# A split-float feed-forward on one NeuronCore: both parts of x in one 512-wide moving operand, the second matrix's operands split on chip

## The chip, the cores and the metric

The program runs on one core of a Trainium2 chip. The metric is the device time of one execution in microseconds (us). The runs of the kernel before took 2144.7, 2146.0 and 2149.2 us; their median, 2146.04 us, is the time before.

## What is computed

One block of a trunk over 512 tokens of width 2048: a projection into four groups of mixers, the mixers, an output projection, and a feed-forward with a squared ReLU. The change lies in the feed-forward and in what borders on it:

```python
x = x + rms_norm(mix @ w_out, norm_mix_post)
h = rms_norm(x, norm_ff_pre)
y = jnp.square(jax.nn.relu(h @ w_ff1)) @ w_ff2        # 2048 -> 8192 -> 2048
x = x + rms_norm(y, norm_ff_post)
```

Everything is float32.

## The kernel before

**Split operands.** Every large product is made from operands that are split in two: `h`, the value rounded to the matmul type (`F32R`), and `l`, the rest. A product of two split operands is three matmuls into one PSUM bank: h times h, h times l, l times h (`mm3`). Splitting takes a cast on ScalarE (`S.copy`) and a subtraction on VectorE.

**Seven products in place of eight.** Each of the two matrices of the feed-forward is multiplied by a Strassen-like scheme: the operands are cut into 2x2 blocks, sums of blocks are made on VectorE (or by accumulating DMAs that GpSimd issues), and seven products p = 1 to 7 are added up into four results. The products are done in the order 1, 5, 6, 2, 7, 3, 4 or close to it; several products go on in a bank where another left off (`PREV`: 6 after 1, 7 after 6, 4 after 7, 3 after 5), once that bank has been read.

**First matrix** (`NU1` = 32 units, about 842 to 1507 us). The weights are the stationary operand, x the moving one. x stands in SBUF as `R` (products 1, 2, 4, 5) and as `S3`, `S6`, `S7` (products 3, 6, 7), with the h part and the l part 256 tokens wide each. One product of one unit is 8 steps of k, and each step is three matmuls with 256 columns: `wh` by x's h, `wh` by x's l, `wl` by x's h. Of the first 16 units the products 1 and 2 are done ahead of the rest (`head_job`, the "heads"); `head_mid` and `head_out` copy the two results to `hst` and send them to DRAM (`stash`). Then come the remaining products (`ffn`, `evac1`); `evac1` squares the ReLU, makes the block sums of y for the second matrix, splits them into h and l, and writes both parts to DRAM (`ydr`, 1792 KB for a unit).

**Second matrix** (`NU2` = 16 units, about 1498 to 2118 us). The parts of y are loaded from `ydr` into regions of `R` (`load_y`, 1024 KB for each product of each pair of units) and are the stationary operand; the weights are the moving one, 512 wide. One product is 24 matmuls. `evac2` adds each finished bank to one of four accumulators (`acc`) on VectorE.

**End.** When a chunk of 512 columns of a token tile is complete, `z_chunk` sums its squares on ScalarE. `final` turns the sum into a factor (`rsq`: VectorE, then a power on GpSimd), multiplies factor and weight row in on VectorE, and adds each chunk to the output in DRAM with an accumulating DMA issued by GpSimd. The residual x had been written to the output earlier, by `x2_tail`.

**What sets the order.** A driver (`Driver`) runs all of this as tasks while the program is built, with a table of instruction costs, and writes an instruction when its task is due. On each engine and each DMA queue the instructions then run in the order written. Weights come as 512 KB blocks through rings of buffers (`V` with three, `X`, `W` and `Z` with two); `mill` adds blocks, casts them to `wh` and subtracts to `wl`, four of each (`NHL`). All helpers record their instructions at line 79, so that the profile tells groups apart by tile names: `R`, `S`, `wh`, `wl`, `raw` (ring V and early weights), `hst`, `ev`, `yt`, `acc`, and `mx` and `pj` for the PSUM banks.

## Time and profile before

| | |
|---|---|
| median of three runs | 2146.04 us |
| the profiled execution, its own time | 2144.77 us |
| its span, first to last instruction | 2142.7 us |
| TensorE busy | 2085.7 us (97%) |
| VectorE busy | 1581.3 us (74%) |
| ScalarE busy | 1071.1 us (50%) |
| GpSimd busy | 218.7 us (10%) |
| DMA, mean | 201 GB/s |

The profile is of one execution. A matmul's row gives its start and a modelled length that reaches into the next one, so the rate of a stream of matmuls is read from the starts of its rows, and a busy share of 97% holds short gaps as well. A row of a table by stretches gives the stretch, its length, and then for TensorE, its weight loads (PEld), VectorE, ScalarE and GpSimd the busy time with the number of instructions; last come the granted TensorE clock as a share of 2.4 GHz, the busy share of the DMA engines, and GB/s. An entry with "x2" or "x4" in a list in order of time is that many instructions in a row, with the time from the first start to the last end. "A <- B" in a list of waits: A sat idle until B ended; the figures are the time in total, the number of waits and the longest.

### The profile page before, as it was taken

How to read it: one execution, taken by the hardware profiler on the slowest of the kernel's cores; microseconds unless marked ns; L12 is line 12 of the kernel's file. 1: busy time of each engine (PE TensorE's matmuls, PEld its weight loads, DVE VectorE, ACT ScalarE, POOL GpSimd, SP SyncE). 2: the span in 40 equal slices, each digit the busy share in tenths (PEclk: the TensorE clock that was granted, in tenths of full speed). 3: DMA queues.
4: the chain of work that ended last, by engine and by line, in shares of the span. 5: the costliest groups of instructions: out<-in, count | busy, mean ns of one | idle time of the engine just before them, and what ended most of it. 6: DMA issues, size and time to landing. Idle time of an engine off the chain costs nothing.

```text
span 2142.7 us, 30890 instructions
## 1 busy us (share of the span) xinstructions
PE 2085.7 (97%) x12100; PEld 1834.5 (86%) x12100; DVE 1581.3 (74%) x2069; ACT 1071.1 (50%) x1530; POOL 218.7 (10%) x280
## 2 busy tenths in 40 slices
PE   9899999999999999989999999999999999999995
PEld 7688888888888888989999999999788888888884
DVE  4655677678765575868888888888667877778775
ACT  6254454465654455645656656656543433433342
POOL 0321121030110000000000000000100100001013
PEclk9999999999999999999999999999999999999998
DMA  8222222222224766677788877788998798789875
GB/s 317 64 90 83 80 74 79 69 79 80 79 79 165 251 227 233 205 247 241 249 252 253 251 243 256 256 258 288 316 310 264 206 305 274 221 256 286 257 209 98
DMA packets 141490, 431.33 MB, mean 201 GB/s; under 512 B 12305, under 2 KB 18721, under 8 KB 136865
## 3 DMA queue, kind: packets, MB, share of 16 engines
q1 hardware_dynamic: 115856, 307.71, 39.9%
q0 software_dynamic: 16128, 54.53, 14.8%
q10 hardware_dynamic: 9360, 67.12, 8.6%
q8 instruction: 95, 1.56, 0.3%
q14 instruction: 51, 0.41, 0.1%
HBM read 358.00 MB, written 71.31 MB: 200 GB/s over the span
## 4 chain that ended last, share of the span: by engine, by line
PE 83%; DMA 5%; DVE 5%; ACT 3%; issue 2%; POOL 1%; SPq 0%; ACTq 0%; POOLq 0%; DVEq 0%
PE mx L79 51%; PE pj L79 32%; DVE wl L79 2%; ACT wh L79 1%; DMA stash<-hst 1%; DMA ydr<-yt 1%; DMA R<-ydr 1%; DVE raw L79 1%; ACT yt L79 0%; DMA raw<-in_w_cv_dram 0%; POOL out_dram L79 0%; DVE yt L79 0%; DMA rsd<-rs 0%; DVE xT L79 0%; DMA wst<-in_ws_t_dram 0%
## 5 line engine op out<-in xcount | busy, mean ns | idle before, releaser
L79 DVE TENSOR_TENSOR wl<-raw,wh 128x1024 fp32r<-128x1024 f32 (+1 forms) x433 | 528.8, 1228 | 332.1 <-ACT wh L79 327.0
L79 ACT CAST wh<-raw 128x1024 fp32r<-128x1024 f32 (+1 forms) x433 | 450.7, 1047 | 574.5 <-DVE raw L79 251.7
L79 PE MATMUL mx<-wh,R 128*128 128x512 f32 x2048 | 644.5, 393 | 7.8 <-ACT wh L79 5.0
L79 PE MATMUL pj<-R,wh 128*128 128x512 f32 (+1 forms) x1888 | 526.3, 362 | 8.7 <-ACT hst L79 8.7
L79 PEld LDWEIGHTS mx<-wh,R 128*128 128x128 f32 x2048 | 387.9, 190 | 88.4 <-ACT wh L79 5.0
L79 PE MATMUL mx<-wl,R 128*128 128x512 f32 x1024 | 402.7, 393 | 1.6 <-DVE wl L79 0.9
L79 PEld LDWEIGHTS pj<-R,wh 128*128 128x128 f32 x1888 | 331.8, 189 | 54.5 <-ACT hst L79 10.6
L79 PE MATMUL pj<-R,wl 128*128 128x512 f32 (+1 forms) x944 | 342.0, 362 | 0.7 <-DVE wl L79 0.7
L79 PE MATMUL mx<-R,wh 128*128 128x256 f32 x1440 | 260.9, 283 | 0.0
L79 PEld LDWEIGHTS mx<-wl,R 128*128 128x128 f32 x1024 | 194.0, 189 | 45.4 <-DVE wl L79 5.1
L79 PE MATMUL mx<-S,wh 128*128 128x256 f32 x1280 | 228.9, 281 | 0.4 <-ACT mx L79 0.4
L79 PEld LDWEIGHTS mx<-R,wh 128*128 128x128 f32 x1440 | 224.5, 192 | 0.0
L79 PE MATMUL mx<-R,wl 128*128 128x256 f32 x720 | 203.9, 283 | 0.0
L79 PEld LDWEIGHTS pj<-R,wl 128*128 128x128 f32 x944 | 178.8, 189 | 23.4 <-DVE wl L79 1.1
L79 PEld LDWEIGHTS mx<-S,wh 128*128 128x128 f32 x1280 | 196.4, 189 | 0.6 <-ACT mx L79 0.6
L79 PE MATMUL mx<-S,wl 128*128 128x256 f32 x640 | 180.4, 282 | 1.2 <-DVE wl L79 1.2
L79 PE MATMUL pj<-wh,R 128*128 128x512 f32 x512 | 162.7, 389 | 0.0
L79 PEld LDWEIGHTS mx<-R,wl 128*128 128x128 f32 x720 | 138.1, 192 | 0.0
L79 DVE TENSOR_TENSOR yt<-yt 128x256 f32<-128x256 f32 (+1 forms) x160 | 113.4, 742 | 32.5 <-ACT yt L79 31.4
L79 POOL DMA_DIRECT2D raw<-in_w_ff_dram x64 | 55.4, 866 | 725.9 <-DVE wl L79 725.9
L79 PEld LDWEIGHTS mx<-S,wl 128*128 128x128 f32 x640 | 120.8, 189 | 2.0 <-DVE wl L79 2.0
L79 PEld LDWEIGHTS pj<-wh,R 128*128 128x128 f32 x512 | 96.1, 188 | 19.9
(292 smaller groups left out, 2462.2 us busy)
## 6 DMA issues: line engine op xcount, KB each, us to landing
ydr<-yt ACTq DMA_DIRECT2D x32, 1792.0 KB, 6.7
R<-ydr SPq DMA_DIRECT2D x56, 1024.0 KB, 10.1
raw<-in_w_ff_dram SPq DMA_DIRECT2D x96, 512.0 KB, 4.6
raw<-in_w_f_dram SPq DMA_DIRECT2D x80, 512.0 KB, 3.3
raw<-in_w_out_dram SPq DMA_DIRECT2D x64, 512.0 KB, 4.1
X<-in_w_ff_dram SPq DMA_DIRECT2D x64, 512.0 KB, 6.2
Z<-in_w_ff_dram SPq DMA_DIRECT2D x64, 512.0 KB, 6.8
raw<-in_w_ff_dram POOLq DMA_DIRECT2D x64, 512.0 KB, 5.8
```

The source lines that it names most:

```text
L79: r = f(*args, **kw)
```

## The change

**First matrix.** `mm1` makes two matmuls of a step instead of three: `wh` by both parts of x, one moving operand of 512 columns (two runs of 256), and `wl` by x's h, 256 columns into the lower half of the bank. A bank so holds two halves that must be added; that is done when it is read (`fold`, and pairs of additions in `evac1`). Because every product now fills a whole bank, results go on in another way: after product 1 its bank is copied by ScalarE into a fresh bank, in which product 2 goes on; after product 6 likewise, with the sign turned, for product 3. A bank that has not yet been written by a matmul gets one first (`seed`). The late product 4 of the unit before now comes after product 6 of a unit, or after product 5 at the first unit of the second matrix, and no longer after its first product.

**Heads.** `head_mid` copies the whole bank (512 columns) to `h1` and sends it off at once; `head_out` folds into `h2` and sends that. `stash` holds three rows for a unit instead of two.

**y.** `ydr` holds y's block sums unsplit (896 KB for a unit, sent in two parts). `load_ys` loads 512 KB for each product into one of two buffers `yr`, in one fixed sequence, the next but one when a buffer has been split; `split_y` casts and subtracts into `R`.

**Weights.** `mill` hands each block to a task of its own (`piece`), so that a block that waits doesn't hold the next ones.

**End.** `z_chunk` multiplies the weight row in at once. In `final`, for the token tiles 0 and 1, ScalarE applies the factor and GpSimd issues the accumulating DMAs as before. For the tiles 2 and 3 the residual is written to a DRAM tile `x2d` early, loaded back into SBUF during the last units (`load_x3`, 1024 KB each), and added on chip, one chunk by ScalarE and GpSimd and three by VectorE; SyncE sends plain writes.

The core of the diff:

```diff
+    x2d = dp.tile([SEQ, D], F32, name="x2d")
...
-            nc.scalar.dma_start(out=out[t * P:(t + 1) * P, c], in_=x2[:, c])
+            nc.scalar.dma_start(out=(out if t < 2 else x2d)[t * P:(t + 1) * P, c], in_=x2[:, c])
...
-        return R[:, hf, hl, off + k, :]
+        return R[:, hf, :, off + k, :]
...
-        seq2 += [(u, todo[0])] + late + [(u, p) for p in todo[1:]]
+        at = todo.index(6) + 1 if u < NU1 else 2
+        seq2 += [(u, p) for p in todo[:at]] + late + [(u, p) for p in todo[at:]]
...
     def mm1(bank, p, k, wh, wl, first, last, on):
-        yield from mm3(bank.t[:, 0:256], wh[:, k, :], wl[:, k, :], op1(p, 0, k), op1(p, 1, k), first, last, on)
+        for low in (True, False) if last else (False, True):
+            if low:
+                T.matmul(out=bank.t[:, 0:256], lhsT=wl[:, k, :], rhs=op1(p, k)[:, 0, :], start=False, stop=False,
+                         skip_group_check=True)
+            else:
+                T.matmul(out=bank.t, lhsT=wh[:, k, :], rhs=op1(p, k), start=first, stop=last, skip_group_check=on)
+            yield PE0
...
+    def fold(dst, bt):
+        S.copy(out=dst, in_=bt[:, 0:256])
+        V.tensor_tensor(out=dst, in0=bt[:, 256:512], in1=dst, op=ALU.add)
...
     def head_mid(u, bank, ev):
         yield ev
-        hst[u] = stage.tile([P, 2, 256], F32, tag="hst", name="hst", bufs=3 if p3 is None else 2)
-        S.copy(out=hst[u][:, 1, :], in_=bank.t[:, 0:256])
+        if p3 is None:
+            x = p2.tile([P, 512], F32, tag="h1", name="h1", bufs=3)
+        else:
+            x = yp.tile([P, 4, 256], F32, tag="yr", name="h1", bufs=2)[:, 0:2].rearrange("p a t -> p (a t)")
+        S.copy(out=x, in_=bank.t)
         hmid[u].fire(drv.cur.time)
+        nc.scalar.dma_start(out=stash[u, :, 1:3, :].rearrange("p a t -> p (a t)"), in_=x)
...
         e, bt = evs[u], banks[u, p][0].t[:, 0:256]
-        if p in (1, 5, 6):
-            S.copy(out=e[:, {1: 0, 5: 1, 6: 2}[p], :], in_=bt)
+        if p in (1, 6):
+            q = {1: 2, 6: 3}[p]
+            yield ("pe", 1)
+            b = Bank()
+            seed(b)
+            banks[u, q] = [b]
+            yield PE0
+            S.activation(out=b.t, in_=bt, func=AF.Copy, scale=1.0 if p == 1 else -1.0)
             mid[u, p].fire(drv.cur.time)
...
-            yh, yl = (y[:, 1:8, hl, :] for hl in range(2))
-            S.copy(out=yh.bitcast(F32R), in_=yl)
-            V.tensor_tensor(out=yl, in0=yl, in1=yh, op=ALU.subtract)
...
+            nc.scalar.dma_start(out=ydr[u, :, 3:7], in_=yb[:, 1:5])
...
+    def load_ys():
+        for n, (b, p) in enumerate(yseq):
+            if n > 1:
+                yield yused[yseq[n - 2]]
+            for u in range(4 * b, 4 * b + 4):
+                yield yfin[u]
+            yield PE0
+            t = yp.tile([P, 4, 256], F32, tag="yr", name="yr", bufs=2)
+            nc.sync.dma_start(out=t, in_=ydr[4 * b:4 * b + 4, :, YI[p]].rearrange("k p t -> p k t"))
+            yraw[b, p] = t
+            ygot[b, p].fire(drv.dma(1 << 19))
+
+    def split_y(b, p, guard):
         yield guard
...
+        S.copy(out=h, in_=t)
+        V.tensor_tensor(out=l, in0=t, in1=h.bitcast(F32), op=ALU.subtract)
+        yload[b, p].fire(drv.cur.time)
+        yused[b, p].fire(drv.cur.time)
...
+        V.tensor_tensor(out=z, in0=z, in1=wfp[:, cs], op=ALU.mult)
...
-            V.scalar_tensor_tensor(out=z, in0=z, scalar=rs, in1=wfp[:, cs], op0=ALU.mult, op1=ALU.mult)
-            G.dma_start(out=out[t * P:(t + 1) * P, cs], in_=z, accum_op=ALU.add)
+            if t < 2:
+                S.activation(out=z, in_=z, func=AF.Copy, scale=rs)
+                yield PE0
+                G.dma_start(out=out[t * P:(t + 1) * P, cs], in_=z, accum_op=ALU.add)
+            elif c == 0:
+                S.activation(out=z, in_=z, func=AF.Copy, scale=rs)
+                G.tensor_tensor(out=z, in0=z, in1=x3s[t][:, cs], op=ALU.add)
+                nc.sync.dma_start(out=out[t * P:(t + 1) * P, cs], in_=z)
+            else:
+                V.scalar_tensor_tensor(out=z, in0=z, scalar=rs, in1=x3s[t][:, cs], op0=ALU.mult, op1=ALU.add)
+                nc.sync.dma_start(out=out[t * P:(t + 1) * P, cs], in_=z)
```

TensorE at the first head of the first matrix, before; `pj` is the bank, `R` holds x, and "x2" stands for two equal instructions:

```order
L79 MATMUL mx<-wh,R 128x512
L79 MATMUL pj<-R,wh 128x256 x2
L79 MATMUL pj<-R,wl 128x256
L79 MATMUL pj<-R,wh 128x256 x2
L79 MATMUL pj<-R,wl 128x256
```

The same place after the change:

```order
L79 MATMUL mx<-wh,R 128x512
L79 MATMUL pj<-R,wh 128x512
L79 MATMUL pj<-R,wl 128x256
L79 MATMUL pj<-R,wh 128x512
L79 MATMUL pj<-R,wl 128x256
```

Two of the three matmuls of a step became one of twice the width; the third stayed.

ScalarE in one unit of the second matrix whose partner unit came before it, that is in every second unit, before:

```order
L79 CAST wh<-raw 128x1024 x8
L79 CAST wh<-W 128x1024 x2
L79 CAST wh<-X 128x1024 x2
L79 CAST wh<-Z 128x1024 x2
L79 CAST wh<-raw 128x1024 x8
```

and after:

```order
L79 CAST wh<-raw 128x1024 x7
L79 CAST R<-yr 128x4x256
L79 COPY mx<-pj 128x512 x2
L79 CAST wh<-W 128x1024
L79 CAST wh<-raw 128x1024
L79 CAST R<-yr 128x4x256
L79 CAST wh<-W 128x1024
L79 CAST wh<-X 128x1024
L79 CAST R<-yr 128x4x256
L79 CAST wh<-X 128x1024
L79 CAST wh<-Z 128x1024
L79 CAST R<-yr 128x4x256
```

The casts of y (`R<-yr`, seven for each pair of units, all in the second one) now stand between the casts of the weights, as does the copy from bank to bank after product 1.

GpSimd at the end, from the power of token tile 2 on, before (`w` and `zs` hold the factor of a token tile, `acc` the chunks, `x` the residual):

```order
L79 TENSOR_TENSOR w_18800<-w_18800,nhalf 128x1
L79 DMA out_dram<-acc_14389 128x512
L79 DMA out_dram<-acc_14390 128x512 x2
L79 DMA out_dram<-acc_14388 128x512 x2
L79 TENSOR_TENSOR w_18820<-w_18820,nhalf 128x1
L79 DMA out_dram<-acc_14390 128x512 x2
L79 DMA out_dram<-acc_14388 128x512 x2
```

and after:

```order
L79 TENSOR_TENSOR zs_7790<-zs_7790,nhalf 128x1
L79 DMA out_dram<-acc_12879 128x512
L79 TENSOR_TENSOR acc_12880<-acc_12880,x_16956 128x512
L79 DMA out_dram<-acc_12879 128x512 x2
L79 TENSOR_TENSOR zs_7791<-zs_7791,nhalf 128x1
L79 TENSOR_TENSOR acc_12880<-acc_12880,x_16958 128x512
```

Of sixteen accumulating DMAs eight are left; behind the power of the last tile GpSimd has one addition where it had four DMAs to issue.

## Rows read from the trace of the kernel before

**Rows 1.** The page: busy time by engine, granted clock, chain that ended last.
```profile
PE 2085.7 (97%) x12100; PEld 1834.5 (86%) x12100; DVE 1581.3 (74%) x2069; ACT 1071.1 (50%) x1530; POOL 218.7 (10%) x280
...
PEclk9999999999999999999999999999999999999998
...
PE 83%; DMA 5%; DVE 5%; ACT 3%; issue 2%; POOL 1%; SPq 0%; ACTq 0%; POOLq 0%; DVEq 0%
```

**Rows 2.** Table by stretches: heads, first matrix, transition, second matrix, end.
```profile
842.00:953.00 111.00, 101.19 (x823) 98.74 (x822) 81.40 (x100) 61.21 (x106) 3.02 (x4) 1.00 0.68 230
953.00:1498.00 545.00, 543.78 (x4559) 543.03 (x4560) 467.37 (x519) 334.23 (x441) 27.82 (x32) 1.00 0.80 252
1498.00:1535.00 37.00, 34.25 (x159) 28.49 (x158) 26.24 (x28) 19.61 (x23) 3.45 (x4) 0.96 1.04 351
1535.00:2107.00 572.00, 571.38 (x2513) 471.20 (x2512) 439.49 (x468) 229.03 (x239) 51.81 (x60) 1.00 0.83 253
2107.00:2142.70 35.70, 11.03 (x49) 8.81 (x47) 16.47 (x31) 5.18 (x13) 17.37 (x20) 0.72 0.71 118
```

**Rows 3.** TensorE in order of time, first matrix: start, length, engine, operation, tiles.
```profile
1100.02 0.40 PE L79 MATMUL mx<-R,wh 128*128 128x256 f32 x2
...
1110.10 0.40 PE L79 MATMUL mx<-R,wh 128*128 128x256 f32 x2
...
1110.46 0.40 PE L79 MATMUL mx<-S,wh 128*128 128x256 f32 x2
...
1118.98 0.40 PE L79 MATMUL mx<-R,wh 128*128 128x256 f32 x2
```

**Rows 4.** TensorE in order of time, projection: x in two runs, 512 wide.
```profile
640.04 0.62 PE L79 MATMUL pj<-R,wh 128*128 128x512 f32 x2
...
651.60 0.62 PE L79 MATMUL pj<-R,wh 128*128 128x512 f32 x2
```

**Rows 5.** Groups of instructions, whole span: count, busy us, mean ns, idle before.
```profile
L79 DVE TENSOR_TENSOR wl<-raw,wh 128x1024 fp32r<-128x1024 f32 (+1 forms) x433 | 528.8, 1228 | 332.1 <-ACT wh L79 327.0 <-DMA Z<-in_w_ff_dram 1.5 <-PE mx L79 1.0
...
L79 DVE TENSOR_TENSOR yt<-yt 128x256 f32<-128x256 f32 (+1 forms) x160 | 113.4, 742 | 32.5 <-ACT yt L79 31.4
...
L79 DVE TENSOR_TENSOR acc<-mx,acc 128x512 f32<-128x512 f32 x120 | 78.2, 685 | 22.3 <-PE mx L79 22.3
...
L79 DVE TENSOR_TENSOR ev<-mx,ev 128x256 f32<-128x256 f32 x48 | 20.1, 420 | 2.9 <-PE mx L79 2.8
```

**Rows 6.** List of waits, 842 to 955 us (heads).
```profile
ACT hst L79 <- DMA stash<-hst: 8.8, 6, 3.3
PE pj L79 <- ACT hst L79: 8.7, 9, 2.5
```

**Rows 7.** Chain that ended last, at the transition: start, length, what.
```profile
1517.42 13.90 DMA R<-ydr
1531.33 0.14 issue
1531.46 12.73 PE mx L79 x48
```

**Rows 8.** DMA issues, whole span: count, size of one, median us to landing.
```profile
R<-ydr SPq DMA_DIRECT2D x56, 1024.0 KB, 10.1
...
Z<-in_w_ff_dram SPq DMA_DIRECT2D x64, 512.0 KB, 6.8
...
out_dram<-x ACTq DMA_DIRECT2D x16, 256.0 KB, 5.1
...
out_dram<-acc POOLq DMA_DIRECT2D x16, 256.0 KB, 7.4
```

**Rows 9.** GpSimd in order of time at the end of the span.
```profile
2123.45 1.58 POOL L79 TENSOR_TENSOR w<-w,nhalf 128x1 f32<-128x1 f32 x1
2126.11 3.57 POOL L79 DMA_DIRECT2D out_dram<-acc  x4 [1.09 <-DVE acc L79]
```

**Rows 10.** Table by stretches, after the last DMA issue.
```profile
2132.00:2136.00 4.00, 0.00 (x0) 0.00 (x0) 0.00 (x0) 0.00 (x0) 0.00 (x0) 0.50 1.07 194
2136.00:2140.00 4.00, 0.00 (x0) 0.00 (x0) 0.00 (x0) 0.00 (x0) 0.00 (x0) 0.50 0.09 16
```

More of the change, by code (lines that the diff above doesn't have):

```diff
@@ L1784, in preload @@
         banks[u, 6] = [b]
-        if (b.kind, b.slot) not in seeded:
-            T.matmul(out=b.t[:, 0:256], lhsT=R[:, 0, 0, 0, 0:P], rhs=R[:, 0, 0, 0, :], start=True, stop=True)
-            yield PE0
-        S.copy(out=banks[u, 6][0].t[:, 0:256], in_=evs[u][:, 2, :])
+        seed(b)
+        yield PE0
+        S.copy(out=b.t, in_=evs[u][:, 1:3, :].rearrange("p a t -> p (a t)"))
         pre6[u].fire(drv.cur.time)
@@ L1884, in evac2 @@
         bs = banks[v, p]
+        if p == 1:
+            yield ("pe", 2)
+            banks[v, 2] = [Bank() for _ in toks]
+            for b2, b1 in zip(banks[v, 2], bs):
+                seed(b2)
+                S.copy(out=b2.t, in_=b1.t)
+            mid[v, 1].fire(drv.cur.time)
+            return
         k, sign = TO[p]
@@ L1948, in ffn @@
                     nc.sync.dma_start(out=wfp, in_=a['w_ff_post'].partition_broadcast(P))
+                if v == NU2 - 2 and p == 6:
+                    for t in (2, 3):
+                        drv.spawn(load_x3(t))
                 cont = PREV.get(p)
@@ L1952, in ffn @@
                     yield pre6[u]
+                elif p == 2 or one and p == 3:
+                    yield mid[u, 1 if p == 2 else 6]
+                    on = True
                 elif on:
```

246 lines of the change are left out of this document (131 added, 115 removed).

## The prediction

> **What bounds the kernel now.** I read the page first, then the table by stretches, then TensorE's starts inside the stretches, and only then the waits. The page says that TensorE is busy for 97% of the span at the full clock, and that 83% of the chain that ended last is its work [rows 1]. The table by stretches says the same of the two matrices of the feed-forward one by one: in the first matrix TensorE is idle for 545.0 - 543.8 = 1.2 us, in the second for 0.6 us [rows 2]. VectorE is the next (86% and 77%), the DMA engines have 80% and 83%. So time is won only where TensorE's own work shrinks, or at the three places where it stands: the heads (111.0 - 101.2 = 9.8 us idle), the transition (2.75 us idle and a clock of 0.96), and the end, where the last matmul is over at 2107 + 11.0 = 2118.0 us and the span runs on to 2142.7 [rows 2].
>
> **The matmuls of the first matrix.** A step is three matmuls of 256 columns. With x from `R`, 28 steps take 1110.10 - 1100.02 = 10.08 us, 360 ns each, so 120.0 ns for a matmul; with x from `S`, 24 steps take 8.52 us, 355 ns each, 118.3 ns for a matmul [rows 3]. A new step is one matmul of 512 and one of 256. The 512-wide form is in the trace, with `wh` stationary and x as two runs of `R`: in the projections 17 steps of three such take 11.56 us, 680 ns each, 226.7 ns for a matmul [rows 4]. That is less than two of 256, although the columns are as many. So the new step costs 226.7 + 120.0 = 346.7 ns from `R`, 13.3 less, and 226.7 + 118.3 = 345.0 from `S`, 10.0 less if the wide form isn't faster there too. 32 units with 7 products of 8 steps are 1792 steps; products 1, 2, 4, 5 use `R` (4/7, 1024 steps), 3, 6, 7 use `S` (768). Gain: 1024 x 13.3 + 768 x 10.0 = 13.6 + 7.7 = **21.3 us**; with 10.0 or 13.3 throughout, 17.9 or 23.8. It counts in full because TensorE waits for nothing there.
>
> The two widths, 120.0 and 226.7 ns, fit 106.7 ns for 256 columns and 13.3 ns fixed for each matmul. The Trainium skill, "TensorE: Matmul & The Clock Gate", section "Back-to-back issue gap", gives N / 2.4 + 2.5 ns for an isolated matmul, which would leave only 2.5 ns to save in a step: 1792 x 2.5 = 4.5 us, and the sum below would end at 2135.5. The trace speaks against it, with 13.3 ns beyond the columns at either width.
>
> **Heads.** Each head's two halves share one `hst` buffer from the first copy to the landing of the DMA. ScalarE waits 8.8 us for these landings, and TensorE 8.7 us for ScalarE's copies [rows 6]. After the change the first copy has its own buffer, sent off at once. But for the last three heads there are two buffers instead of three, and ScalarE copies 512 columns. What is late next are the casts of weights, since the tail of the output projection runs on the same engines (VectorE 73% here [rows 2]). I take **3 us**; bounds: all 8.7 us, and -3 us if the shared `yr` buffers hold the copies longer than `hst` did.
>
> **Transition.** The page's chain has a 1024 KB load of y that lands after 13.9 us; then 48 matmuls take 12.7 us instead of 48 x 226.7 = 10.9 [rows 4, 7]. With 2.9 us of standing (the idle 2.75 us and an issue) that is 4.7 us, in a stretch where the DMA engines are saturated (1.04 [rows 2]). Half the bytes of y must now be loaded. But the loads go through two buffers, the next but one only after a split, and the casts stand in ScalarE's queue in front of weights and of the copy for product 3. I take **2 us**; bounds 4.7 and -3.
>
> **VectorE.** In the first matrix it loses 32 subtractions of 1792 columns and gains 128 additions of 256 columns (in `evac1` and `fold`). The `yt` group is 160 instructions in 113.4 us, of which 128 are 256-wide; at 0.42 us these are 53.8, so the 32 wide ones are 59.6 us. The 128 new ones at 0.42 are 53.8 [rows 5]. So its load stays: 467 - 6 of 527 us, 87%. In the second matrix it gains 56 splits of 1.23 us (68.7) and loses 32 additions of 0.685 (21.9), as product 2 goes on where 1 ended: 439.5 + 46.8 = 486 of 572 us, 85%. But the splits fall into every second unit. A unit lasts 7 x 24 x 226.7 ns = 38.1 us; there VectorE has 29.3 us on average now, and 29.3 + 7 x 1.23 - 1.4 = 36.5 us after, 96%. Four buffers of split weights (two products) stand between it and TensorE, so I count no steady loss. ScalarE gains as many casts and 80 copies, and stays at some 60% of either matrix or below.
>
> **New waits.** Product 2 now waits for ScalarE's copy of product 1's bank, with product 5 (about 2.8 us) between; behind that copy stand the casts of the next weights, and ahead of it may stand a cast that waits for VectorE's addition. Product 3 waits likewise for product 6, with the late product 4 between in most units. These are 48 copies. Before, product 7 waited for the copy of 6 with one product between, at no visible cost [rows 2]. I take **-2 us** for all new waits in both matrices; bounds 0 and -10.
>
> **End.** Before: the last power on GpSimd ends at 2125.0, the four DMA issues behind it at 2129.7 [rows 9]; the transfers are at full load until 2136 and over soon after [rows 10], and 6 us more end the program. An accumulating DMA lands after 7.4 us, a plain one of the same size after 5.1 [rows 8]. After: the last power has on GpSimd three DMA issues, one power and one addition ahead of it, on VectorE three multiply-adds instead of four multiplications, so it comes at about the same time. Behind it stand three VectorE operations of some 0.7 us and plain writes, which would land near 2125.0 + 2.2 + 5.1 = 2132.3, or one addition of GpSimd later. Against 2136.5 that is some 3 to 4 us; I take **3 us**; bounds 7 (nothing queues) and -3 (GpSimd's additions and issues in front of the last power come late). The multiplications by the weight row, moved ahead, add 16 x 0.69 = 11 us to VectorE in the last two units, which have no splits: 34 to 35 of 38.1 us each, hidden.
>
> **Sum.** 21.3 + 3 + 2 - 2 + 3 = 27.3 us. The profiled execution took 2144.8 (its span 2142.7 and 2.1 around it) and would take 2117.5. The median is 1.3 us above it; so **2118.7 us**.
>
> **Rivals.**
>
> (a) Only the matmuls count: the stops at heads, transition and end stay or are replaced by others, and the tighter chain from bank to bank costs 5 us: 2146.0 - 21.3 + 5 = 2129.7. For it: three engines share queues that got longer; against it: the stops have causes that the change takes away by name.
>
> (b) The change doesn't do what it says: the 13.3 ns belong to the columns (768 in a step, as before) and not to the matmul, because a weight load that follows a narrow matmul keeps some of its time uncovered. Then the step stays at 360 ns, and 27.3 - 21.3 = 6 us remain: 2140.0. Against it: both widths are measured with a weight load for each matmul.
>
> (c) All stops go: 23.8 + 8.7 + 4.7 + 7 = 44.2: 2102.
>
> (d) Slower: y's loads hold ScalarE. Two buffers let load n start when split n-2 is done, two products of 5.4 us earlier, 10.9 us. If a load, waiting in SyncE's queue included, takes L longer than that, ScalarE stands in front of its cast with the weights' casts behind, and TensorE loses L - 10.9 for each two splits, 24.5 times in the seven pairs of units that are split in the second matrix. The gain is gone at L = 10.9 + 27.3 / 24.5 = 12.0 us; at 13 the time is 2118.7 + 2.1 x 24.5 = 2170. For it: 1024 KB of y took 10.1 us; against it: now it is 512 KB, and such blocks land in 6.8 [rows 8].
>
> **How the numbers follow.** Forecast (2110 to 2125) 0.58; (a), 2125 to 2137, 0.20; (c), below 2110, 0.09; (b), with cases in which new waits eat most of the gain, 0.07; (d) 0.06. The range from 2105 to 2135 leaves out (b), (d) and the outer parts of (a) and (c), about 0.2. What a measurement of this kernel can tell from no change is some 0.2%, 4.3 us. Faster by more: 0.58 + 0.20 + 0.09 and half of (b), 0.90; within 0.04; slower 0.06.
>
> **What would show it.** Starts of the new steps in the first matrix 345 to 347 ns apart (360 means (b)); the first matrix some 18 us shorter at the same few us of idle TensorE; at the transition no long wait for y; in the second matrix TensorE without gaps also in the units with splits, and no wait of ScalarE for `yr` above 1 us there (that would be (d)); GpSimd's last power near 7 us after the last matmul and the transfers over some 14 us after it. The prediction is wrong if TensorE shows idle time behind copies from bank to bank.

## The result and the profile after

The changed kernel takes 2176.03 us (median of four runs, 2174.75 to 2180.34), the kernel before 2146.03 us in the same session: a ratio of 1.0141, 95% interval 1.0123 to 1.0159. It is 30 us slower; 27 us faster had been predicted.

The page of the changed kernel, busy time and chain (as in [rows 1]):

```profile
PE 2090.7 (96%) x10306; PEld 1748.0 (80%) x10306; DVE 1616.4 (74%) x2211; ACT 1141.1 (53%) x1644; POOL 214.2 (10%) x274
...
PE 81%; DVE 7%; ACT 5%; DMA 3%; issue 3%; POOL 0%; ACTq 0%; SPq 0%; DVEq 0%; POOLq 0%
```

The busy shares hardly move, and would not show the loss; only the chain does, with 7% on VectorE and 5% on ScalarE, where it had 5% and 3%. The table by stretches of the changed kernel, cut as in [rows 2], shows it:

```profile
842.00:953.00 111.00, 94.39 (x494) 80.05 (x493) 76.79 (x105) 58.77 (x95) 2.13 (x4) 0.92 0.71 225
953.00:1498.00 545.00, 530.89 (x2990) 457.36 (x2989) 444.57 (x603) 320.67 (x451) 27.00 (x31) 1.00 0.68 201
1498.00:1535.00 37.00, 31.22 (x155) 25.80 (x154) 31.27 (x38) 22.44 (x30) 2.60 (x3) 0.93 0.79 220
1535.00:2107.00 572.00, 560.91 (x2460) 460.41 (x2459) 464.97 (x479) 285.14 (x307) 50.17 (x58) 1.00 0.79 214
```

TensorE was idle for 9.8, 1.2, 2.75 and 0.6 us in these four; now it is 16.6, 14.1, 5.8 and 11.1 us, and the clock of the heads is 0.92. VectorE and ScalarE aren't fuller than forecast, and the DMA engines have less to do. So nothing is saturated; TensorE waits where it did not. (The stages of the changed kernel end up to 23 us later than these cuts, so a row of it holds some of the stage before.)

To see where each stage ends, the starts of four matmuls of the changed kernel: the first of the heads, the first with x from `S`, the first of the second matrix, the last one:

```profile
841.45 0.39 PE L79 MATMUL pj<-R,wh 128*128 128x512 f32 x1
...
970.81 0.40 PE L79 MATMUL mx<-S,wh 128*128 128x512 f32 x1
...
1521.01 0.39 PE L79 MATMUL mx<-wh,R 128*128 128x512 f32 x1
...
2154.69 0.39 PE L79 MATMUL pj<-wh,R 128*128 128x512 f32 x1
```

The same four stand at 841.43, 952.84, 1498.44 and 2117.64 in the kernel before. This gives the lengths of the stages, read in the same way from each kernel's profiled execution; the second matrix counts to the end of the last matmul, 0.39 us after its start:

| us | heads | first matrix | second matrix | end | sum |
|---|---|---|---|---|---|
| before | 111.4 | 545.6 | 619.6 | 24.7 | 1301.3 |
| after | 129.4 | 550.2 | 634.1 | 17.9 | 1331.6 |
| difference | +18.0 | +4.6 | +14.5 | -6.8 | +30.3 |

What is ahead of the heads is the same code in all kernels here, and ends between 839.7 and 844.0 us from one profiled execution to another; a stage's difference of 1 or 2 us means nothing.

**Heads.** From the list of waits of the changed kernel, ScalarE's and TensorE's for the addition of `h`, 842 to 955 us (total, number, longest):

```profile
ACT wh L79 <- DVE h L79: 11.6, 8, 3.0
...
PE pj L79 <- DVE h L79: 8.4, 5, 2.6
```

One case, ScalarE in order of time:

```profile
861.85 0.37 ACT L79 COPY h<-pj 128x256 f32<-128x256 f32 x1
864.90 0.33 ACTq L1711 DMA_DIRECT2D stash<-h  x1
865.26 1.04 ACT L79 CAST wh<-raw 128x1024 fp32r<-128x1024 f32 x1 [3.04 <-DVE h L79]
```

`fold` copies half the bank on ScalarE (861.85), VectorE adds the other half when its turn comes (its addition starts at 864.45), and the DMA issue written directly behind waits for it in ScalarE's queue. So the next cast of weights is 3.04 us late. The bank, too, is free only after that addition. TensorE, 15 us on:

```profile
881.01 0.80 PE L79 MATMUL pj<-R,wh 128*128 128x512 f32 x1 [2.61 <-DVE h L79]
...
881.82 0.63 PE L79 MATMUL pj<-R,wh 128*128 128x512 f32 x1
...
882.46 0.63 PE L79 MATMUL pj<-R,wh 128*128 128x512 f32 x1
```

After the stop the steps are 0.64 us apart (881.82 to 882.46), where a step takes 0.35 at the full clock.

**Second matrix.** A pair of units takes 78.5 us, 76.6 before; it stops once, in the unit with splits. All engines of the changed kernel in order of time there:

```profile
2049.39 1.04 ACT L79 CAST R<-yr 128x1024 fp32r<-128x1024 f32 x1
...
2050.34 1.05 ACT L79 CAST wh<-W 128x1024 fp32r<-128x1024 f32 x1
...
2050.47 1.23 DVE L79 TENSOR_TENSOR R<-yr,R 128x1024 fp32r<-128x1024 f32 x1 [1.01 <-ACT R L79]
2051.61 1.28 DVE L79 TENSOR_TENSOR acc<-mx,acc 128x512 f32<-128x512 f32 x2
...
2052.81 1.21 DVE L79 TENSOR_TENSOR wl<-raw,wh 128x1024 fp32r<-128x1024 f32 x1
...
2054.08 0.50 PE L79 MATMUL pj<-wl,R 128*128 128x512 f32 x1 [1.75 <-DVE wl L79]
```

The split of y stands ahead of the weight piece that TensorE needs next. VectorE is idle for 1.01 us in front of it, while the cast for `wl` is done. All of them, in the lists of waits from 1540 to 2110 us:

```profile
ACT R L79 <- PE pj L79: 60.1, 29, 3.5
DVE R L79 <- ACT R L79: 48.7, 50, 2.1
ACT R L79 <- PE mx L79: 20.1, 14, 1.4
PE pj L79 <- DVE wl L79: 11.1, 7, 1.8
```

ScalarE's cast waits for TensorE's last matmul on the region that it overwrites, not for y (no wait for `yr<-ydr` is among them; these DMAs land in 4.8 us). The region isn't needed again before the next unit, 38 us later. The order makes the least urgent work the first.

### The profile page after: what moved, and what is told of

It reads as the page before. It is cut to its first block, busy times and chain, and to the rows that moved or that the text cites. A ratio compares the mean times of both kernels' runs of the same rounds, so it can differ in the third digit from the quotient of the medians.

```text
span 2173.0 us, 27681 instructions
## 1 busy us (share of the span) xinstructions
PE 2090.7 (96%) x10306; PEld 1748.0 (80%) x10306; DVE 1616.4 (74%) x2211; ACT 1141.1 (53%) x1644; POOL 214.2 (10%) x274
## 4 chain that ended last, share of the span: by engine, by line
PE 81%; DVE 7%; ACT 5%; DMA 3%; issue 3%; POOL 0%; ACTq 0%; SPq 0%; DVEq 0%; POOLq 0%
PE mx L79 50%; PE pj L79 31%; DVE wl L79 3%; ACT wh L79 2%; ACT ev L79 1%; ACT R L79 1%; ACT ya L79 1%; DVE acc L79 0%; DMA raw<-in_w_cv_dram 0%; DMA rsd<-rs 0%; DVE ev L79 0%; DVE yw L79 0%; DVE xT L79 0%; DVE R L79 0%; DMA yr<-ydr 0%
## 5 line engine op out<-in xcount | busy, mean ns | idle before, releaser
L79 PE MATMUL pj<-R,wh 128*128 128x512 f32 x1584 | 530.9, 403 | 15.1 <-DVE h L79 8.4
L79 PEld LDWEIGHTS pj<-R,wh 128*128 128x128 f32 x1584 | 297.1, 190 | 73.1 <-DVE h L79 10.2
L79 PE MATMUL mx<-R,wh 128*128 128x512 f32 x720 | 257.4, 397 | 0.6 <-ACT wh L79 0.6
L79 PE MATMUL mx<-S,wh 128*128 128x512 f32 x640 | 228.9, 397 | 0.7 <-ACT mx L79 0.7
L79 PE MATMUL mx<-R,wl 128*128 128x256 f32 x720 | 187.9, 281 | 1.9 <-DVE wl L79 1.9
L79 PE MATMUL mx<-S,wl 128*128 128x256 f32 x640 | 167.5, 282 | 6.1 <-DVE wl L79 6.1
L79 PEld LDWEIGHTS mx<-R,wh 128*128 128x128 f32 x720 | 134.1, 189 | 24.9 <-ACT wh L79 0.9
L79 PEld LDWEIGHTS mx<-S,wh 128*128 128x128 f32 x640 | 118.8, 188 | 22.2 <-ACT mx L79 1.0
L79 PE MATMUL pj<-wl,R 128*128 128x512 f32 x256 | 100.4, 392 | 11.1 <-DVE wl L79 11.1
```

The source lines that it names most:

```text
L79: r = f(*args, **kw)
```

## The experiments

All ran with the kernel before on the same chip; ratios are to that, with the 95% interval. Times of single stages come from each kernel's profiled execution.

| kernel | median us | ratio to before | heads | first m. | second m. | end |
|---|---|---|---|---|---|---|
| after | 2176.0 | 1.0141 (1.0123 to 1.0159) | 129.4 | 550.2 | 634.1 | 17.9 |
| y_late | 2157.2 | 1.0062 (1.0047 to 1.0077) | 126.0 | 551.4 | 616.2 | 17.6 |
| heads_late | 2170.3 | 1.0121 (1.0106 to 1.0136) | 123.6 | 552.3 | 634.8 | 17.7 |
| heads_bank | 2167.5 | 1.0109 (1.0094 to 1.0124) | 118.7 | 551.0 | 632.1 | 18.0 |
| heads_old | 2163.3 | 1.0095 (1.0079 to 1.0112) | 116.2 | 554.2 | 630.1 | 17.6 |
| narrow | 2177.0 | 1.0150 (1.0135 to 1.0165) | 126.9 | 557.6 | 630.5 | 17.3 |
| relu_gap | 2260.2 | 1.0546 (1.0530 to 1.0562) | 128.8 | 642.7 | 631.8 | 18.6 |
| plan_clock | 2165.9 | 1.0106 (1.0091 to 1.0121) | 124.4 | 544.9 | 635.6 | 17.7 |
| no_fold | 2162.9 | 1.0094 (1.0077 to 1.0111) | 125.6 | 540.9 | 634.4 | 18.2 |
| yl_hb | 2156.7 | 1.0060 (1.0045 to 1.0075) | 121.9 | 553.8 | 618.2 | 17.8 |
| yl_hb_pc | 2144.3 | 1.0004 (0.9995 to 1.0014) | 121.7 | 547.5 | 613.6 | 18.2 |
| yl_ho_rg | 2237.4 | 1.0433 (1.0416 to 1.0451) | 115.1 | 639.1 | 615.8 | 17.8 |
| yl_ho_pc | 2139.8 | 0.9983 (0.9973 to 0.9992) | 115.0 | 547.2 | 616.3 | 17.5 |
| best_pair | 2137.3 | 0.9962 (0.9948 to 0.9977) | 115.1 | 539.4 | 619.0 | 18.0 |
| end_only | 2135.3 | 0.9956 (0.9939 to 0.9972) | 111.7 | 546.4 | 618.9 | 17.3 |
| before_clock | 2144.5 | 1.0006 (0.9996 to 1.0016) | | | | |

`pair_order` and `wide_both` ran once, for their traces.

### The split's place: y_late

```diff
                     if v % 2:
-                        yfree[b, p].fire(drv.pe + 0.15)
+                        yfree[b, p].fire(drv.pe + 3.0)
```

> The changed kernel, with one number altered: in the second matrix the split of a part of y (cast on ScalarE, subtraction on VectorE) is written 2.85 us later in the planner's time, so that it stands behind the weight pieces that come next and TensorE is done with the region when its turn comes. Work and bytes are the same. Theory P (the place in the queues): in the changed kernel the cast waits for TensorE's last matmul on the region and holds ScalarE and VectorE in front of weights; TensorE stops once in each pair of units, 1.75 to 2 us, seven times. P expects these stops gone, a pair of units at 76.6 to 77.0 us instead of 78.5, and 2163 us (2161 to 2167) instead of 2176. Rival A (the amount: VectorE simply has too much to do in a unit with splits, whatever the order): the stops stay or move to another product, 2174 to 2178.

0.8% less than the changed kernel, some 17 us where P expected 13, and the second matrix is 17.9 us shorter, below the kernel before; a pair of units takes 76.2 us. Of the four waits shown above one is left, in the list of waits of y_late over the same stretch:

```profile
DVE R L79 <- ACT R L79: 2.8, 2, 2.1
```

The work is the same. So it was the place (P), and not VectorE's load (A).

### Emptying the heads: heads_late, heads_bank, heads_old

```diff
         bank.free()
+        drv.cur.time += 2.0
+        yield PE0
         nc.scalar.dma_start(out=stash[u, :, 0, :], in_=x)
```

> The changed kernel, with the DMA issue of the second head result (h2 to the stash) written 2 us later on ScalarE's queue, behind casts of weights, and no longer directly behind the fold whose addition on VectorE it waits for. Theory Q (a wait in ScalarE's queue): in the changed kernel ScalarE stands up to 3 us for VectorE's addition in front of these issues, the casts of weights behind it come late, TensorE stops for 2 to 3 us at a time and its granted clock falls. Q expects the clock between 862 and 982 us back above 0.97, the first product of the first unit after the heads 12 to 16 us earlier, and 2160 to 2164 us. Rival B (the heads lose because the fold and the wider copies are more work on VectorE and ScalarE than before): 2171 to 2177.

Less than half of what theory Q expected: the heads are 5.8 us shorter, not 12 to 16, the whole 2 in 1000, and the clock between 862 and 982 us is 0.94 (0.91 in the changed kernel), not above 0.97. The DMA issue is one cause only; TensorE still waits for the bank behind VectorE's addition (6.5 us in the list of waits). The next kernel frees the bank by a copy:

```diff
-            x = p2.tile([P, 256], F32, tag="h2", name="h2", bufs=2)
+            x = p2.tile([P, 512], F32, tag="h2", name="h2", bufs=2)
...
-        fold(x, bank.t)
+        S.copy(out=x, in_=bank.t)
         bank.free()
-        nc.scalar.dma_start(out=stash[u, :, 0, :], in_=x)
+        yield PE0
+        V.tensor_tensor(out=x[:, 0:256], in0=x[:, 256:512], in1=x[:, 0:256], op=ALU.add)
+        drv.cur.time += 1.0
+        yield PE0
+        nc.scalar.dma_start(out=stash[u, :, 0, :], in_=x[:, 0:256])
```

> The changed kernel; only the second evacuation of a head is altered: ScalarE copies the whole bank (512 columns) and the bank is free at once; VectorE adds the halves later, from SBUF, and the DMA issue comes 1 us behind that. Three buffers of h1 become two, so that the memory stays the same. Theory Q2 (the bank is held): with the DMA issue moved (heads_late) the heads still took 12 us more than in the kernel before, because the next head's bank is free only after VectorE's addition has had its turn; expects the stage from the first head matmul to the first product from S at 114 to 119 us (129 in the changed kernel, 111 before) and 2162 to 2168 us. Rival B (amount of work and a low granted clock, whatever is held): 122 us or more there, 2171 to 2176.

118.7 us, as Q2 expected (114 to 119): the held bank counts. But TensorE now waits 13.2 us for the copies of `h`, one of which waited for the landing of an earlier DMA. Undoing the heads altogether:

```diff
-                yield from mm1(banks[u], p, k, wh, wl, p == 1 and k == 0, k == 7, p == 2)
+                yield from mm3(banks[u].t[:, 0:256], wh[:, k, :], wl[:, k, :], op1(p, k)[:, 0, :], op1(p, k)[:, 1, :],
+                               p == 1 and k == 0, k == 7, p == 2)
```

(with `head_mid` and `head_out` of the kernel before)

> The changed kernel with the heads undone: three matmuls of 256 columns for a step, one ScalarE copy of 256 columns for each of the two results, one buffer and one DMA for both, as before; the copy that opens product 6 of such a unit fills the upper half of the bank with zeros. All else as changed. Theory H (the heads' loss of 18 us comes from how the heads are emptied and is theirs alone): the stage at 111 to 113 us, 2156 to 2161 us. Rival C (the heads are only where a loss shows that lies elsewhere, in weights that come late or in the stage behind, which then gets longer): 2166 or more.

Between the two: 13.2 of the 18 us are the heads' own; 5 us stay although the heads' own instructions are those of before, and the first matrix is 4 us longer. In these heads ScalarE waits 10.8 us for the landings of `hst` (8.8 before), TensorE stops once for 3.0 us, and the clock is 0.92 and 0.93 from 902 to 942 us, where it was 1.00. What brings that about was not settled; the tail of the output projection, which runs beside the heads, still differs (one buffer `junk2` for two), and was not tried.

### The matmuls of the first matrix: narrow, no_fold, pair_order, wide_both

In the first matrix the kernel repeats itself every two units, 12 products, 96 steps. ScalarE's ReLU of the units marks it. Two starts, one period apart, of the kernel before, then of the changed kernel, then of no_fold:

```profile
1204.94 0.84 ACT L79 ACTIVATE ev<-ev 128x768 f32<-128x768 f32 x1
...
1239.23 0.85 ACT L79 ACTIVATE ev<-ev 128x768 f32<-128x768 f32 x1
```

```profile
1191.62 0.84 ACT L79 ACTIVATE ev<-ev 128x768 f32<-128x768 f32 x1
...
1226.21 0.84 ACT L79 ACTIVATE ev<-ev 128x768 f32<-128x768 f32 x1
```

```profile
1185.54 0.84 ACT L79 ACTIVATE ev<-ev 128x768 f32<-128x768 f32 x1
...
1219.53 0.84 ACT L79 ACTIVATE ev<-ev 128x768 f32<-128x768 f32 x1
```

Over all periods the usual ones are 34.30, 34.57 and 33.97 us. They hold 48 steps with x from `R` and 48 with x from `S`. First the edit that undoes the wide matmul alone:

```diff
-                T.matmul(out=bank.t, lhsT=wh[:, k, :], rhs=op1(p, k), start=first, stop=last, skip_group_check=on)
+                for hl in range(2):
+                    T.matmul(out=bank.t[:, 256 * hl:256 * hl + 256], lhsT=wh[:, k, :], rhs=op1(p, k)[:, hl, :],
+                             start=first, stop=last, skip_group_check=True)
+                drv.pe -= 0.0135
```

(This kernel doesn't compute the whole block: both halves of a bank are opened with a start of their own.)

> The changed kernel, with the 512-wide matmul of each step of the first matrix made as two of 256 columns, into the two halves of the bank; the planner counts the same time, so the order and all else stay. Theory M (the wide matmul saves 6 to 9 ns in each of 1792 steps, and the stops that the change adds are another matter): 1792 x 6 to 9 = 11 to 16 us more, 2187 to 2192. Rival N (in the first matrix the stops are the saving given back: ScalarE's and VectorE's chains set the pace, and TensorE only waits for less when it is slower): 0 to 5 us more, 2176 to 2181.

2 us more than the changed kernel in all, the number of rival N, but only in small part for its reason: the period grew by 0.41 us to 34.98, and the stage by 7.4, while the heads and the second matrix came out 2.5 and 3.6 us shorter. The wide matmul does save time, and less than I took. How much, TensorE without stops must tell:

```diff
         S.copy(out=dst, in_=bt[:, 0:256])
-        V.tensor_tensor(out=dst, in0=bt[:, 256:512], in1=dst, op=ALU.add)
+        if p3 is None:
+            V.tensor_tensor(out=dst, in0=bt[:, 256:512], in1=dst, op=ALU.add)
+        else:
+            drv.account("V", 0.1 + 256 * 0.00107)
```

> The changed kernel, with part of the computation left out: in the first matrix, from the opening of the rings on, the additions of a bank's two halves in fold (products 2, 4, 5 and the last heads, about 83 of 0.42 us on VectorE) are not made; the planner still counts them, so the places of all else stay. Theory V (the new additions, and VectorE's waits for the ScalarE copies ahead of them, are what makes weights late there): the 13 us of stops in the first matrix fall to 4 or less, 2163 to 2167 us. Rival L2 (the stops come from the casts' place behind activations and copies on ScalarE, which stays): 2170 to 2176 us.

The stops are nearly gone, as theory V expected. The table by stretches from 1100 to 1500 us, changed kernel and then no_fold:

```profile
1100.00:1500.00 400.00, 393.33 (x2227) 339.70 (x2226) 330.26 (x457) 237.82 (x335) 19.88 (x23) 1.00 0.70 205
```

```profile
1100.00:1500.00 400.00, 399.49 (x2259) 344.61 (x2258) 317.29 (x399) 245.10 (x343) 20.68 (x24) 1.00 0.69 208
```

6.7 us idle in 400 there, 0.5 here, by leaving out some 60 additions of 0.42 us (VectorE's busy time falls by 13 us in this stretch).

One pause in each period is left, and the busy time hides it behind the modelled lengths. It is at the first step of product 6 in the units without heads, where the first matmul with `wl` waits for VectorE. TensorE there, in the changed kernel and then in no_fold, and VectorE's subtraction in no_fold:

```profile
1231.12 0.40 PE L79 MATMUL pj<-S,wh 128*128 128x512 f32 x1
1232.12 0.39 PE L79 MATMUL pj<-S,wl 128*128 128x256 f32 x1 [0.60 <-DVE wl L79]
1232.35 0.39 PE L79 MATMUL pj<-S,wh 128*128 128x512 f32 x1
```

```profile
1224.44 0.40 PE L79 MATMUL pj<-S,wh 128*128 128x512 f32 x1
1224.84 0.39 PE L79 MATMUL pj<-S,wl 128*128 128x256 f32 x1
1225.07 0.40 PE L79 MATMUL pj<-S,wh 128*128 128x512 f32 x1
```

```profile
1223.56 1.23 DVE L79 TENSOR_TENSOR wl<-raw,wh 128x1024 fp32r<-128x1024 f32 x1 [1.00 <-ACT wh L79]
```

Such a step takes 1.23 us in the changed kernel and 0.63 in no_fold, where 0.35 is usual: pauses of 0.87 and 0.28 us. Without them the periods are 33.70 and 33.69 us, so TensorE at its own pace makes a step in 351 ns, against 34.30 / 96 = 357.3 before: 6 ns saved, not 12.

The saving isn't the same for both sources of x. The changed kernel at the start of 24 steps from `R` (which end at 1231.12, above), and at the start and the end of 16 from `S`:

```profile
1222.74 0.40 PE L79 MATMUL pj<-R,wh 128*128 128x512 f32 x1
...
1237.56 0.40 PE L79 MATMUL mx<-S,wh 128*128 128x512 f32 x1
...
1243.19 0.39 PE L79 MATMUL mx<-R,wh 128*128 128x512 f32 x1
```

That is 349 ns from `R` and 352 from `S`, against 360 and 355 before [rows 3]. The means of all steps without a pause between 1050 and 1480 us are 349.9 and 352, against 359.4 and 355.1: 9.5 ns saved from `R`, where I had 13.3, and 3 from `S`, where I had 10.0. The next two kernels, planned with 33.97 / 96 = 353.9 ns, which holds the pause, ask where the rest is.

```diff
+        if k < 6:
+            todo = (wide, k, k + 1) if k % 2 == 0 else (narrow, k - 1, k)
+        else:
+            todo = (narrow, 6, 7) if k == 6 else (wide, 6, 7)
+        for q in todo[1:]:
+            todo[0](q)
+            yield PE0
```

(`wide` and `narrow` are the two matmuls of `mm1`; no_fold's edit is in it too)

> no_fold (the additions of the two halves left out, so that TensorE doesn't stop in the first matrix) with the matmuls of two steps in another order: wide, wide, narrow, narrow instead of wide, narrow, wide, narrow. Read from it: the time of a pair of units in the first matrix, 96 steps, 33.97 us in no_fold, 353.9 ns for a step. Theory W (each change of width costs: 354 where 346.7 were added up, for two changes in a step): half as many changes, 350 ns and 33.6 us or less. Rival X (the wide matmul itself is dearer here, or the weight load of a narrow one isn't covered): 33.9 to 34.0 us as before.

The period is 33.65 us, 350.5 ns for a step, as theory W expected, but W isn't shown by it. The same place as above:

```profile
1223.55 0.63 PE L79 MATMUL pj<-S,wh 128*128 128x512 f32 x2
1224.02 0.44 PE L79 MATMUL pj<-S,wl 128*128 128x256 f32 x2
```

Two wide matmuls now stand ahead of the first with `wl`, which is needed 0.23 us later and is there (VectorE's subtraction for it ends at 1223.89). So 0.28 of the 0.32 us that the period lost are the pause. Against the pace of 351 ns, 6 changes of width in a product in place of 14 give back some 0.5 ns for a step.

```diff
-                T.matmul(out=bank.t[:, 0:256], lhsT=wl[:, k, :], rhs=op1(p, k)[:, 0, :], start=False, stop=False,
-                         skip_group_check=True)
+                T.matmul(out=bank.t, lhsT=wl[:, k, :], rhs=op1(p, k), start=False, stop=False, skip_group_check=True)
```

> The changed kernel with both matmuls of a step 512 wide (the low part of the weights meets both parts of x, which adds a product that the reference's accuracy doesn't need). TensorE has 30% more to do in the first matrix, so the other engines have time and it should not stop. Read from it: the time of 96 steps. If a 512-wide matmul costs 226.7 ns here too, as in the projections, 453.4 ns and 43.5 us (theory W: without width changes nothing is added). Rival X: the wide one costs 232 to 234 ns here, 464 to 468 ns and 44.5 to 44.9 us.

44.27 us, 461.1 ns for two, 230.6 ns for a wide matmul: between the two, because it is the mean of two sorts. The starts of a stretch of 48 matmuls from `R`, of 16 from `S`, and of the next:

```profile
1223.80 0.39 PE L79 MATMUL pj<-R,wh 128*128 128x512 f32 x1
...
1234.70 0.40 PE L79 MATMUL pj<-S,wh 128*128 128x512 f32 x1
...
1238.44 0.39 PE L79 MATMUL mx<-R,wh 128*128 128x512 f32 x1
```

From `R` the wide matmul costs 227 ns, about what it costs in the projections, which read `R` too; from `S` it costs 234. With a narrow one of the kernel before (120.0 and 118.3 [rows 3]) that makes some 347 and 352 ns, and steps take 349.9 and 352. So with `S` the wide form itself is dearer, and with `R` 3 ns are lost in the mix of widths. Why, wasn't found.

### The order in the first matrix: relu_gap, plan_clock, before_clock

```diff
+            drv.cur.time += 1.5
             yield PE0
             S.activation(out=e, in_=e, func=AF.Relu)
+            drv.cur.time += 1.5
             yield PE0
```

> The changed kernel; in the first matrix the ReLU and the square of a unit's three results are written 1.5 us later each, behind casts of weights on ScalarE. Theory L (the order of ScalarE's queue): in the changed kernel ReLU, square and a DMA issue stand ahead of two casts, VectorE stands 1.3 to 1.7 us for these casts, and TensorE loses 6 to 7 us in each 400 us; expects half of that or less, the stage from the first product from S to the second matrix 4 to 8 us shorter, 2167 to 2172 us. Rival V (VectorE is simply too full for the shorter steps): the stops move elsewhere, 2173 to 2177.

This theory fell, and hard: 85 us more. The buffer `ev` is now free some 3 us later, the next unit's load from the stash lands later, and ScalarE's copy of it into the bank for product 6 stands in the queue with the casts behind. The list of waits of relu_gap, 970 to 1500 us (16.0 in the changed kernel), and a stretch:

```profile
ACT mx L79 <- DMA ev<-stash: 56.1, 13, 5.0
```

```profile
1200.00:1300.00 100.00, 86.64 (x448) 73.38 (x447) 70.74 (x99) 50.02 (x71) 4.32 (x5) 0.90 0.56 170
```

TensorE idle for 13 us in 100, and its clock at 0.90. The load had become longer by the change already, 384 KB in 4.2 us for 256 KB in 3.1, which leaves the less room.

The planner (`cost_t`) counts 347 ns for a step that takes 351 without pauses (360 with them, 34.57 / 96), so it believes TensorE further ahead than it is, and writes evacuations too early; ScalarE stands 126 us for TensorE between 970 and 1500 us, 31 before.

```diff
                 T.matmul(out=bank.t, lhsT=wh[:, k, :], rhs=op1(p, k), start=first, stop=last, skip_group_check=on)
+                drv.pe += 0.006
```

> The changed kernel; the planner counts 6 ns more for each step of the first matrix (353 instead of 347 ns; the trace shows 348 to 354). Work is the same, only places in the queues move. Theory K (the planner's TensorE is ahead of the real one, so that evacuations are written too early and ScalarE stands for TensorE with casts behind: 126 us of such waits between 953 and 1540 us in the changed kernel, 31 before): expects these waits below 80 us, about half of the 13 us of stops in the first matrix gone, and 2166 to 2171 us. Rival V (the stops come from VectorE's work and its chain with ScalarE's casts, whatever the planner counts): 2172 to 2177 us.

7 to 8 us less; ScalarE's waits for TensorE are 84 us (a little above the 80 of theory K), and the period is 34.08 us: the pause is down from 0.87 to 0.40 us. The first matrix is 5 us shorter, and so are the heads, whose steps are counted in the same place. Theory K holds in the main. With no_fold, which takes most of the pause away while ScalarE's waits for TensorE stay (130 us), it shows that VectorE's new additions and the wrong places both have a part in the stops. The cross-check on the kernel before, which doesn't have the additions:

```diff
         yield from mm3(bank.t[:, 0:256], wh[:, k, :], wl[:, k, :], op1(p, 0, k), op1(p, 1, k), first, last, on)
+        drv.pe -= 0.006
```

> The kernel before, with one number altered: the planner counts 6 ns less for each step of the first matrix than it takes (354 instead of 360), the error that it has in the changed kernel. Work is the same. Theory K in its general form (a planner that is ahead of TensorE makes stops by itself): ScalarE's waits for TensorE in the first matrix rise from 31 us to over 80, TensorE stops for 5 to 8 us more, 2149 to 2154 us. Rival K2 (the kernel before has the slack for it; the error costs only where VectorE's additions already make weights late): 2143 to 2147 us.

No difference (K2): there the slack covers the planner's error. ScalarE's waits were not read in it, so only the time tells.

### The end alone, and combinations

The kernel before with `x2d`, and `z_chunk`, `final` and `load_x3` of the changed kernel:

```diff
-            nc.scalar.dma_start(out=out[t * P:(t + 1) * P, c], in_=x2[:, c])
+            nc.scalar.dma_start(out=(out if t < 2 else x2d)[t * P:(t + 1) * P, c], in_=x2[:, c])
```

> The kernel before, with the new end alone: weight row multiplied in early, factor applied on ScalarE, the residual of token tiles 2 and 3 loaded back and added on chip, plain writes from SyncE for these. Theory E (the end's gain is its own): the last matmul stays at 2118, the tail after it goes from 24.7 to about 18 us, 2139 us (2138 to 2141). Rival F (in the kernel before the loads of the residual and the sixteen early multiplications disturb the last units): 2142 to 2147.

0.44% faster than the kernel before, the tail 17.3 us, the other stages as they were: the end's gain is its own (E). The time is below the 2138 to 2141 us expected; the kernel before took 2144.5 beside it, and the tail is 7.4 us shorter where 7 were expected.

The first combinations, made of the edits above:

> y_late and heads_bank together. If the two losses are apart from each other: 17.5 + 5.7 = 23 us less than the changed kernel, 2149 to 2153 us, still behind the kernel before by what the first matrix doesn't give. If they are not: 2156 or more.

Not so: 2156.7, as much as y_late alone. The heads are 4 us shorter than in y_late, the two stages behind them together as much longer. With the planner's clock mended:

> y_late, heads_bank and plan_clock together. Theory K expects 4 to 8 us less than y_late with heads_bank, 2142 to 2148 us, which is the time of the kernel before; rival V the same as y_late with heads_bank, 2149 to 2154 us.

12 us less, more than theory K expected, and the time of the kernel before.

> y_late, heads_old and relu_gap together. If the three causes are apart from each other their gains add up: 17.5 for the splits' place, some 17 for the heads, some 5 for the order in the first matrix, and 2134 to 2139 us come out, below the kernel before by the gain at the end and a little of the matmuls'. If they are not (a stop that is taken away only brings the next one forward): 2145 or more.

It contains relu_gap, whose 90 us in the first matrix it shows again; its heads and its second matrix are as short as in heads_old and y_late.

> y_late, heads_old and plan_clock together: the splits written later, the heads as in the kernel before, the planner counting 353 ns for a step. If the heads' remaining loss is their own: 3 to 6 us less than with heads_bank in place of heads_old (which came to the time of the kernel before), 2137 to 2142 us, and faster than the kernel before by 0.1 to 0.3%. If the first units of the first matrix only get longer in exchange (they did by 4 us in heads_old): 2142 to 2146.

2139.8, as expected, 0.17% below the kernel before. Last, with the order of pair_order:

> yl_ho_pc with the matmuls of two steps in the order wide, wide, narrow, narrow, and the planner counting 351 ns for a step. If TensorE sets the pace there: 34.13 us for 96 steps become 33.8, and 4 to 5 us of the whole, 2134 to 2137 us. If the stops behind VectorE and ScalarE take it back: 34.1 us again and 2138 to 2142.

The period is 33.63 us: TensorE sets the pace in the first matrix, with the whole computation done. Here too nearly all that the order gives is the pause (0.41 us in yl_ho_pc, 34.13 a period). 0.38% below the kernel before, level with end_only. By stages the first matrix is 6.2 us shorter than before and the end 6.7, the heads 3.7 longer. So the wide matmul does pay in the first matrix, but as a whole the kernel is no faster than with the new end alone.

Not tried by themselves were the tasks of `piece`, the copies from bank to bank and the new place of product 4.

## Why the prediction was wrong, step by step

**The matmuls (21.3 us).** The mechanism, two matmuls cheaper than three, was right; the size was nearly twice too large. In all 1792 steps it is 1024 x 9.5 + 768 x 3 ns, about 12 us. The step that failed is the price of a new step: I added 226.7 ns, measured with x from `R` in a stream of wide matmuls, to the price of a narrow one, for `R` and for `S`. From `S` the wide matmul takes 234 ns (wide_both), so of the 10.0 ns only 3 are left; from `R` a step of both widths takes 3 ns more than the sum. The condition stood in the prediction ("if the wide form isn't faster there too"), but only in the one direction. Rival (b), a step as long as before, didn't happen. The Trainium skill, "TensorE: Matmul & The Clock Gate", section "Back-to-back issue gap", gives N / 2.4 + 2.5 ns for an isolated matmul, by an estimate 109.2 ns for 256 columns, 215.8 for 512 and 2.5 ns saved in a step. I set it aside because its single durations don't fit [rows 3, 4]; those measured here don't fit it either (118 to 120 and 227 to 234 ns), but the 6 ns measured lie between its saving and mine.

**Heads (+3 us).** Wrong in sign: 18 us lost, beyond my bound of -3, although the matmuls should save some 2.4 there (256 steps x 9.5 ns). I named the casts as next in line and ScalarE's wider copies, and did not see that `fold` puts VectorE, 73% full there, between a bank and its release, and that the DMA issue behind it waits in ScalarE's queue. The diff showed both. heads_late and heads_bank put 6 and 11 of the 18 us down to these two, heads_old 13 to all that was changed in the heads; 5 us stay open.

**Transition (+2 us).** No gain: in the 37 us from the first matmul of the second matrix on (1521 to 1558 us), TensorE is idle for 3.8 us at a clock of 0.91, against 2.75 at 0.96. y is not what it waits for any more; two stops of 0.9 and 2.9 us come behind weight pieces.

**VectorE ("I count no steady loss").** The loads were right (445 of 545 us, 465 of 572; I had 461 and 486), the step from 96% and four buffers to "no steady loss" was not. A buffer of weights helps only if the queue hands them out in the order of need. The splits, in ScalarE's and VectorE's queues ahead of weights, cost 14.5 us in the second matrix, and none of it is load (y_late). I had set this out for y that comes late, as rival (d), but looked at the DMA as what the cast waits for, and not at the other guard, TensorE's last use of the region.

**New waits (-2 us, at worst -10).** In the first matrix the stops, read from the starts, took 16.8 us, 2.4 before: 14 us, beyond the bound, most of it the 0.87 us in each of 16 periods. Not the copies from bank to bank, as I thought (TensorE waits 0.7 us for them), but VectorE's additions together with a planner that counts 347 ns for a step of 351 (no_fold, plan_clock). The 9.7 us that the matmuls save in this stage were lost to it: the stage is 4.6 us longer.

**End (+3 us).** Right in direction, at its upper bound: 6.8 us. GpSimd's last power ends 6.7 us after the last matmul, as forecast (about 7). That power in order of time, and the table by stretches behind it, changed kernel:

```profile
2160.59 1.19 POOL L79 TENSOR_TENSOR zs<-zs,nhalf 128x1 f32<-128x1 f32 x1
```

```profile
2168.00:2170.00 2.00, 0.00 (x0) 0.00 (x0) 0.00 (x0) 0.00 (x0) 0.00 (x0) 0.50 0.79 304
2170.00:2173.00 3.00, 0.00 (x0) 0.00 (x0) 0.00 (x0) 0.00 (x0) 0.00 (x0) 0.50 0.01 5
```

The power before ended at 2125.0 [rows 9], 7.0 us after its last matmul. The transfers, too, are over about where I put them, some 14.5 us after the last matmul (2169.6, an estimate from the DMA share of the first of these rows). What was mis-sized is the rest: 6 us from the last transfer to the end of the program before, against 2136.5, and 3.4 now. Why it is shorter after plain writes, no run tells.

**The sum.** The matmuls gave about 12 us and the end 6.8; the heads took 20, the waits of the first matrix 14 and the second matrix 14.5: 30 us slower.

**The chances.** 0.06 for slower was the real error. I gave it to one mechanism, and had left out the common root of four: new work on VectorE or ScalarE, written by a planner, in queues whose order decides.

## What to carry to other kernels

Where engines work through queues in a fixed order, a forecast of their load is no forecast of waits: for each instruction that a change adds, ask what it waits for and what stands behind it in its own queue, and write the work that is needed last, last. After a change to the instructions that set the pace, correct the durations that the planner counts with; 6 ns a step were worth 8 us here, once the slack was gone. Take the cost of a mix of instructions from a stream of that mix and with the operands' own tiles, and read pauses from the starts: a busy share of nearly 100% hid one of 0.28 us in each period, which would have passed for the cost of the mix. If a change has several parts, time the safest one alone first: the end by itself made a faster kernel.

## What the runs showed of the hardware

A 512-wide matmul with two runs of x takes 226.7 ns in the projections [rows 4]; in the first matrix it takes 227 ns with x from `R` and 234 with x from `S` (wide_both). A step of a wide and a narrow one takes 349.9 and 352 ns; the order wide, wide, narrow, narrow takes some 0.5 ns off a step (351 to 350.5, pair_order).

In the heads of the kernel before, stops of up to 2.5 us leave the granted clock at 1.00 [rows 2, 6]. In the changed kernel the heads have stops of up to 3.7 us, several of them above 2; behind the one that ends at 881.0 the granted clock is 0.50, the lower of its two levels (1.2 GHz), and steps take 0.64 us for 0.35, and stretches of 20 us come down to 0.83:

```profile
881.00:884.00 3.00, 2.99 (x9) 2.61 (x10) 1.56 (x2) 2.64 (x4) 0.00 (x0) 0.50 0.13 44
902.00:922.00 20.00, 15.41 (x69) 13.12 (x70) 11.46 (x14) 10.06 (x14) 0.00 (x0) 0.83 0.62 199
```

Whether the length of the stops or their distance decides, no run here tells apart.
